# First expert stage: a quarter of the tokens by gathered expert rows, the rest dense with a token-stationary second product

## The chip, the cores and the metric

The kernel runs on one core of a Trainium2 chip. The metric is the device time of one execution in microseconds, as a median of runs; one execution was also recorded by the hardware profiler. PE is the tensor engine, DVE is VectorE, ACT is ScalarE, POOL is GpSimd, SP is SyncE, whose queue issues most transfers.

## The reference

Two blocks are computed in a row. The first has two layers over 256 context tokens and 256 latent tokens of width 1024; the second has four layers over 16 + 256 tokens and is not touched. Each layer of the first block ends with a product-key expert network (PEER). For a token h it picks 16 experts in each of 8 heads, 128 rows out of 16384, with softmax gates, and adds up their contributions:

```python
qr = (h @ wq).reshape(b, t, 8, 2, 128)
scores = einsum('bthpd,hpkd->bthpk', qr, subkeys)
s1, i1 = top_k(scores[..., 0, :], 16); s2, i2 = top_k(scores[..., 1, :], 16)
top, pos = top_k(s1[..., :, None] + s2[..., None, :], 16)   # over the 256 sums
eidx = take(i1 * 128 + i2, pos); gate = softmax(top)
act = gelu(einsum('ted,td->te', u[eidx], h))
y = einsum('te,ted->td', gate * act, v[eidx])
```

u and v have 16384 rows of 1024 numbers each. The first layer does this for 512 tokens, the second for 256.

## The kernel before

Activations lie transposed: features on the 128 partitions, tokens along the row, as eight chunks of 128 features. Products are exact to float32: each weight tile `[128, 1024]` is loaded (`wraw`), split into a high part (`whi`, ACT, L202) and a remainder (`wlo`, DVE, L269), the tokens are split likewise into `xh` and `xl`, and three matmuls (high by high, high by low, low by high) are added up in PSUM.

The expert network of a layer is the function `peer`. It is dense: all 16384 experts are computed for all tokens, as 128 groups j of 128 experts, and a gate of zero stands for an expert that was not chosen. It has two parts.

*Routing* (`route`) makes queries and scores on PE, picks the 16 largest on DVE (`choose`), normalises the gates (`gates`), and spreads them over all experts (`spread`): for each token two one-hot matrices are built on DVE (`oa`, `ob`) and multiplied on PE, with the gate in three bf16 parts in the first layer and in one float32 part in the second; the result goes to an array `G` in DRAM. The generator yields the assumed PE and DVE time of each step, and `peer` fills in whole groups of the first product (`u_act`) wherever DVE is assumed to be ahead. These early groups go to an array `U` in DRAM (108 of 128 in the first layer, 124 in the second).

*The dense stage* walks over pairs of groups. `u_phase` fetches gates (`gt`) and stored products (`ad`), or computes a late group itself, applies GELU and gate, and splits the result (`wt`). `v_phase` loads two tiles of v, splits them into `vh` and `vl`, and multiplies with v as the stationary operand and 512 tokens moving: 8 output chunks x 2 groups x 3 parts. In the first layer four output chunks stay in PSUM (the tag `SM`) for the whole stage and four are made in the rotating banks (`MM`) and added to an accumulator in SBUF by DVE (L948). `u_phase` of a pair comes ahead of `v_phase` of the pair before. One row of 1024 modulation weights rides along per pair (`extra`, the function `mods`, DVE at L396) until they are done. A tile scheduler sets the order on each engine; each engine takes its queue in order.

Of the kernel before, what the change touches and what calls it, by code (L numbers as in the profile page):

```python
# [10 lines left out]
F32 = mybir.dt.float32  # L11
# [51 lines left out]
class Big:  # L63
    """chunks x [128, n] in 8 KB pieces."""
# [14 lines left out]
class Kern:  # L79
    def __init__(self, tc, st, A):  # L80
# [7 lines left out]
        self.gdram = [self.dr.tile([P, n // GT, P, GT], F32, name=f"g{n}") for n in (512, 256)]  # L88
        self.udram = [self.dr.tile([P, P, n], F32, name=f"u{n}") for n in (512, 256)]
# [11 lines left out]
    # ---------------------------------------------------------------- constants  # L101
    def consts(self):
# [39 lines left out]
        # -1e30 where column > row; where row > column; off the causal part of the 16-blocks  # L142
# [22 lines left out]
        # hsel[p, h]: 1 at p = h, 32 + h, 64 + h, 96 + h  # L165
# [6 lines left out]
        # hsel16[p, h]: 1 at p = h of every 16  # L172
# [6 lines left out]
        # csel[:, 15 - r:31 - r]: ones in column r of 16  # L179
# [28 lines left out]
    def sigmoid(self, out, z):  # L208
        """1 / (1 + exp(-z))"""
# [52 lines left out]
    def load_w(self, src):  # L262
        """A weight tile [128, n <= 1024] as an exact sum of two float32r parts."""
# [12 lines left out]
    def linear(self, wap, kc, xh, xl, cols, mts, consume, order=None, after=None):  # L276
        """out^T[m-tile] = W[:, m-tile]^T @ x for x^T = xh + xl, [128, kc, tokens]."""
# [15 lines left out]
    def rsq(self, src, n, tag="t", v=None, out=None, eps=None):  # L293
        """(src / n + eps) ** -0.5; v: a tile to reuse; eps: by token"""
# [13 lines left out]
    def root(self, v, l, r):  # L308
        """v ** -0.5 in r; l: to work in"""
# [19 lines left out]
    def norm(self, x, cols, parts, xh, xl, off=0, sums=None):  # L329
        """parts: (a, b, gain [128, 8], shift [128, 8] or None) over column ranges of x."""  # L330
# [16 lines left out]
    # ---------------------------------------------------------------- block 1  # L347
# [10 lines left out]
    def mods(self, l, groups, wt="wmod", jt="j"):  # L358
        """groups: (stream, modulation index) pairs: self.mod[l, s, i] -> [128, 8] columns, tile by tile."""
# [48 lines left out]
    def lower(self):  # L408
        """lower bounds of layer 1: (p0 + p1) - p0 of the softmax over the layers."""
# [16 lines left out]
    def forget(self, l, d, h, ps, b, key):  # L426
        """forget gate of direction d, head h: decay sums b within 128-blocks and the key."""
# [3 lines left out]
        # without a lower bound the floor of the gate is a bound on z  # L431
# [17 lines left out]
    def transposed(self, src, out, blks=None, tag="SM"):  # L449
        """out[t, blk, 128] <- src [128, N] transposed by token blocks."""  # L450
# [14 lines left out]
    def att_levels(self, d, q, k, b, nb, att, levels, tag="SM"):  # L465
        """att[i][s, (h, t)] off the diagonal for direction d, level by level; q, k, b: [128, H, n] in nb blocks."""
# [35 lines left out]
    def state_step(self, d, k, b, blk, vn, S, Snew):  # L502
        """Snew = exp(b_last) S + (k exp(b_last - b))^T v over one block."""
# [1389 lines left out]
```

## Time and profile before

| | |
|---|---|
| median of 3 runs | 4804.88 us (4804.5 to 4808.62) |
| profiled execution: span | 4797.2 us |
| the median above that span | 7.7 us |
| PE busy | 4635.6 us, 97% |
| DVE busy | 3518.2 us, 73% |
| ACT busy | 2207.3 us, 46% |
| POOL busy | 1.0 us |
| moved by DMA | 797.59 MB, mean 166 GB/s |

By stage: the first layer's routing lies from about 340 to 1185 us of the span, its dense stage to 2036, the second layer's mixer to 2260, its routing to 2745, its dense stage to 3135, and the second block after that. Matmuls overlap: the duration of one is longer than its slot in a stream of them, so a slot is read from the starts of a series. Busy time in a stretch is counted once where instructions overlap.

### The profile page before, as it was taken

The numbers are of one execution on the slowest core, as the hardware profiler recorded it, in microseconds if no ns is written. First come the engines' busy times: TensorE is split into PE (matmuls) and PEld (weight loads), VectorE is DVE, ScalarE is ACT, GpSimd is POOL, SyncE is SP. The second block draws the span as 40 slices with busy tenths as digits, with TensorE's granted clock in tenths as the row PEclk, the third lists the DMA queues.
The fourth block names the chain that finished last, engine by engine and source line by source line (L and its number), as shares of the span: only waits on it lengthen the run. The fifth ranks groups of instructions, "written<-read, shape, count | busy, mean of one in ns | idle before, by whom it ended". The sixth has DMA issues, their size and how long they took to land.

```text
span 4797.2 us, 78132 instructions
## 1 busy us (share of the span) xinstructions
PE 4635.6 (97%) x30559; PEld 4149.6 (87%) x30559; DVE 3518.2 (73%) x6655; ACT 2207.3 (46%) x3847; POOL 1.0 (0%) x8
## 2 busy tenths in 40 slices
PE   7999899999999999999999999999999999999999
PEld 5887788888777778878999999978998998899799
DVE  9977998898887775487966866677557567566765
ACT  4443233334333332365445555577445454445853
POOL 0000000000000000000000000000000000000000
PEclk9999999999999999999999999999999998999999
DMA  5423345456867764224577788733553553055255
GB/s 191 131 69 99 102 173 179 167 181 234 263 222 229 228 204 133 80 74 132 182 224 233 265 294 275 239 95 102 173 157 99 174 160 106 15 173 167 89 167 172
DMA packets 317218, 797.59 MB, mean 166 GB/s; under 512 B 26272, under 2 KB 142368, under 8 KB 306608
## 3 DMA queue, kind: packets, MB, share of 16 engines
q1 hardware_dynamic: 316848, 792.60, 50.9%
q8 instruction: 239, 3.92, 0.3%
q14 instruction: 131, 1.07, 0.1%
HBM read 696.28 MB, written 95.94 MB: 165 GB/s over the span
## 4 chain that ended last, share of the span: by engine, by line
PE 77%; DVE 11%; DMA 6%; issue 3%; ACT 3%; SPq 0%; DVEq 0%; ACTq 0%
PE MM L287 32%; PE MM L868 21%; PE SM L942 10%; DMA wraw<-wmodT 4%; PE SM L830 3%; PE MM L942 2%; DVE vl L274 2%; PE A L490 2%; DVE wlo L269 1%; DMA ad<-u 1%; PE PO L1233 1%; DVE b L948 1%; DVE wt L274 1%; DVE j L396 1%; ACT whi L202 1%
## 5 line engine op out<-in xcount | busy, mean ns | idle before, releaser
L202 ACT ACTIVATE whi<-wraw 128x1024 fp32r<-128x1024 f32 (+2 forms) x796 | 831.5, 1046 | 1315.3 <-PE MM L868 650.1
L269 DVE TENSOR_TENSOR wlo<-wraw,whi 128x1024 fp32r<-128x1024 f32 (+2 forms) x796 | 956.0, 1202 | 311.0 <-ACT whi L202 223.2
L868 PE MATMUL MM<-b,whi 128*128 128x512 f32 (+1 forms) x4096 | 1015.9, 339 | 3.6 <-ACT whi L202 3.6
L287 PE MATMUL MM<-xhl,whi 128*128 128x272 f32 (+1 forms) x4736 | 936.4, 294 | 3.2 <-ACT xhl L202 1.6
L287 PE MATMUL MM<-b,whi 128*128 128x272 f32 (+2 forms) x3712 | 851.6, 323 | 50.4 <-ACT b L202 45.3
L287 PEld LDWEIGHTS MM<-xhl,whi 128*128 128x128 f32 x4736 | 752.8, 190 | 24.3 <-issue 10.5
L868 PEld LDWEIGHTS MM<-b,whi 128*128 128x128 f32 x4096 | 700.5, 190 | 81.7 <-ACT whi L202 5.4
L287 PEld LDWEIGHTS MM<-b,whi 128*128 128x128 f32 x3712 | 621.7, 192 | 105.5 <-ACT b L202 51.7
L868 PE MATMUL MM<-b,wlo 128*128 128x512 f32 (+1 forms) x2048 | 693.3, 339 | 13.9 <-DVE wlo L269 13.8
L287 PE MATMUL MM<-xhl,wlo 128*128 128x272 f32 (+1 forms) x2368 | 690.4, 292 | 2.1 <-DVE wlo L269 2.0
L942 PE MATMUL SM<-wt,vh 128*128 128x256 f32 (+1 forms) x3072 | 689.1, 320 | 2.1 <-ACT wt L202 2.1
L287 PE MATMUL MM<-b,wlo 128*128 128x272 f32 (+2 forms) x1856 | 596.8, 322 | 7.9 <-DVE wlo L269 7.5
L942 PEld LDWEIGHTS SM<-wt,vh 128*128 128x128 f32 x3072 | 515.3, 192 | 43.4 <-ACT wt L202 2.3
L942 PE MATMUL SM<-wt,vl 128*128 128x256 f32 (+1 forms) x1536 | 490.8, 320 | 0.0
L287 PEld LDWEIGHTS MM<-xhl,wlo 128*128 128x128 f32 x2368 | 450.0, 190 | 9.8 <-issue 4.7
L202 ACT ACTIVATE vh<-wraw 128x1024 fp32r<-128x1024 f32 x256 | 266.6, 1050 | 403.6 <-PE MM L942 260.3
L868 PEld LDWEIGHTS MM<-b,wlo 128*128 128x128 f32 x2048 | 388.9, 190 | 59.3 <-DVE wlo L269 17.5
L274 DVE TENSOR_TENSOR vl<-wraw,vh 128x1024 fp32r<-128x1024 f32 x256 | 310.3, 1220 | 124.7 <-ACT vh L202 124.6
L287 PEld LDWEIGHTS MM<-b,wlo 128*128 128x128 f32 x1856 | 355.4, 192 | 33.2 <-DVE wlo L269 12.3
L942 PE MATMUL MM<-wt,vh 128*128 128x512 f32 x1024 | 319.0, 393 | 26.5 <-DVE b L948 26.3
L942 PEld LDWEIGHTS SM<-wt,vl 128*128 128x128 f32 x1536 | 294.6, 192 | 20.7
L824 DVE SCALAR_TENSOR_TENSOR ob<-iotab,b,gp 128x384 bf16<-128x384 bf16 x512 | 282.2, 610 | 19.9 <-PE SM L830 19.9
(470 smaller groups left out, 5407.1 us busy)
## 6 DMA issues: line engine op xcount, KB each, us to landing
wraw<-uT SPq DMA_DIRECT2D x256, 512.0 KB, 3.6
wraw<-v SPq DMA_DIRECT2D x256, 512.0 KB, 4.6
wraw<-w_gate_up SPq DMA_DIRECT2D x176, 512.0 KB, 3.5
g<-b SPq DMA_DIRECT2D x48, 1024.0 KB, 6.0
wraw<-w_in SPq DMA_DIRECT2D x64, 512.0 KB, 3.5
gt<-g SPq DMA_DIRECT2D x32, 1024.0 KB, 7.3
wraw<-fox_w_in SPq DMA_DIRECT2D x64, 512.0 KB, 3.5
wraw<-w_down SPq DMA_DIRECT2D x64, 512.0 KB, 3.5
```

Source lines behind the costliest of these rows:

```text
L202: r = nc.scalar.activation(out, in_, func, **kw)
L269: nc.vector.tensor_sub(lo[:, :n], raw[:, :n], hi[:, :n].bitcast(F32))
L274: self.nc.vector.tensor_sub(lo, src, hi.bitcast(F32))
L287: nc.tensor.matmul(ps, w_, x_[k, slice(a, b)], start=(i == 0 and q == 0), stop=(i == kc - 1 and q == 2))
L396: q = nc.vector.scalar_tensor_tensor(j, w, 1.0, self.cond[:, s, :], op0=OP.mult, op1=OP.mult, accum_out=self.mod[l, s, i][:, k:k + 1])
L490: nc.tensor.matmul(p[:w, h * w:(h + 1) * w], xx, xx, start=True, stop=True)
L824: nc.vector.scalar_tensor_tensor(b_, iota[:, None, :].to_broadcast([P, parts, P]), i2T[:, t_], gp[:, :, t_].to_broadcast([P, parts, P]), o ...
L830: nc.tensor.matmul(pg[:, i * P:(i + 1) * P], a[:, i], b_[:, q], start=(q == 0), stop=(q == parts - 1))
L868: nc.tensor.matmul(ps, w_[:, k * P:(k + 1) * P], x_[k, slice(0, N)], start=(k == 0 and q == 0), stop=(k == KD - 1 and q == 2))
L942: nc.tensor.matmul(ps, w_[:, jj, c * P:(c + 1) * P], x_[:, jj], start=first, stop=end, skip_group_check=not own and N < 512)
L948: nc.vector.tensor_add(accs[c - 4, slice(0, N)], accs[c - 4, slice(0, N)], ps)
L1233: nc.tensor.matmul(po[rows, a:b], vn[:c1 - c0, ci * P + 64 * e:ci * P + 64 * e + 64], pT[:c1 - c0, ci * P:ci * P + w], start=(ci == 0), st ...
```

## The change

In the first layer 128 of the 512 tokens (the first 128 context tokens) leave the dense path (`FETCHED = (1, 0)`). For them `gates` computes the expert number i1 x 128 + i2 and keeps it with the gate (`fetch`); no one-hot matrices are made. In the dense stage `tokens_first` turns these tokens so that a token lies on a partition (`H`), and `fetched` goes over the 128 chosen experts of each token: POOL gathers for the 128 partitions the rows of u and v (one array `uv0` with both side by side, 8 KB a row) into one of five tiles `uv`; DVE forms the dot product of u and H with an accumulator (L874); ACT applies GELU and the gate; DVE adds the weighted v row to `o` (L867). Two such experts go with each pair of groups.

The other 384 tokens stay dense. `spread` uses the float32 one-hot form in both layers. In both layers the second product is turned: the tokens (`wt`) are stationary, 128 at a time, and 512 columns of v move; all of the output stays in PSUM for the whole stage (six banks in the first layer, four in the second), the accumulator in SBUF goes, and at the end the result is copied out, transposed on PE and added to x (`add`). v is read from the new array, where the rows of neighbouring partitions are 1 MiB apart instead of 512 KiB. `MM` has two banks instead of three, `wt` two buffers instead of three in the first layer's dense stage, and v's split shares the buffers `whi` and `wlo`, now three each. Comments were taken out, which moves line numbers. Code for a second layer with one dense tile (`whole`) isn't reached with these settings.

```diff
+FETCHED = (1, 0)
-WORKP = dict(nbig=2048, bufs=4, ga=3, w=(5, 2, 2), mm=3, sm=5)
-ROUTE = dict(bufs=8, t=4, gp=1, r=16, alt=2, oa=4, ob=12)
-DENSE = dict(bufs=1, gt=2, ad=2, vh=2, vl=2, wt=3)
+WORKP = dict(nbig=2048, bufs=4, ga=3, w=(5, 3, 3), mm=2, sm=6, sp=4)
+ROUTE = dict(bufs=7, t=4, r=16, alt=2, oa=4, ob=8)
+DENSE = dict(bufs=1, gt=2, ad=2, wt=2, o=2)
+OWN = dict(uv=5, H=1, ir=1)
...
+                if t < nf:
+                    fetch(t, *sels[t], g)
...
-                            nc.vector.scalar_tensor_tensor(
-                                b_, iota[:, None, :].to_broadcast([P, parts, P]), i2T[:, t_],
-                                gp[:, :, t_].to_broadcast([P, parts, P]), op0=OP.is_equal, op1=OP.mult)
...
+                        nc.vector.tensor_scalar(b_, self.iotaf, i2T[:, t_], gT[:, t_], op0=OP.is_equal, op1=OP.mult)
+                        nc.tensor.matmul(pg[:, i * P:(i + 1) * P], a[:, i], b_, start=True, stop=True)
...
+    def fetched(self, l, H, ids, g, acc):
...
+        def out(b):
+            for j in range(b, b + B):
+                v = uv.pop(j)[:, D:]
...
+                    nc.vector.scalar_tensor_tensor(acc, v, w[:, j:j + 1], acc, op0=OP.mult, op1=OP.add)
+                yield
+        for b in range(0, P, B):
+            for j in range(b, b + B):
+                z = uv[j] = self.t(2 * D, tag="uv")
+                nc.gpsimd.indirect_dma_start(z, None, self.A[f"uv{l}"],
+                                             bass.IndirectOffsetOnAxis(ap=ids[:, j:j + 1], axis=0))
+                nc.vector.scalar_tensor_tensor(self.t(D, BF, tag="ga"), z[:, :D], 1.0, H, op0=OP.mult, op1=OP.mult,
+                                               accum_out=act[:, j:j + 1])
...
+            self.actv(act[:, bs], act[:, bs], AF.Gelu)
...
+                self.actv(w[:, j:j + 1], act[:, j:j + 1], AF.Copy, scale=g[:, j:j + 1])
+            if b:
+                yield from out(b - B)
+        yield from out(P - B)
...
-        res = [self.ps() for _ in range(4)]
-        accs = self.big(4, 512) if N == 512 else None
+        res = [[self.ps() for _ in range(2)] for _ in range(nd)]
...
-                nc.sync.dma_start(raw, A["v"][l, :, j0 + jj, :])
-                self.split(raw, vh[:, jj], vl[:, jj])
...
+                nc.sync.dma_start(raw, A[f"uv{l}"].rearrange("(p j) d -> p j d", j=P)[:, j, D:])
...
+                for q, ws, v in ((0, (wh, wl), vh), (1, (wh,), vl)):
+                    for c in range(nd):
+                        for h in range(2):
+                            for i, w_ in enumerate(ws):
+                                nc.tensor.matmul(res[c][h], w_[:, jj, c * P:(c + 1) * P], v[:, h * 512:(h + 1) * 512],
+                                                 start=(j == 0 and q == 0 and i == 0), stop=(j == P - 1 and q == 1))
...
+                for _ in range(J):
+                    next(steps, None)
```

DVE in the first layer's dense stage, in the middle of the early pairs. Before, one pair: products with the gates (`ad`), remainders of v (`vl`) and of the weights (`wt`), the modulation work (`ga`, `mod`), and the additions to the accumulator in SBUF (`b`).

```order
L274 TENSOR_TENSOR vl<-wraw,vh 128x1024
L274 TENSOR_TENSOR wt<-ad,wt 128x1024
L274 TENSOR_TENSOR vl<-wraw,vh 128x1024
L396 SCALAR_TENSOR_TENSOR ga,mod_12740<-wraw,cond 128x1024
L396 SCALAR_TENSOR_TENSOR ga,mod_12741<-wraw,cond 128x1024
L948 TENSOR_TENSOR b_11290<-b_11290,MM 128x512
L918 TENSOR_TENSOR ad<-ad,gt 128x512 x2
L948 TENSOR_TENSOR b_11290<-b_11290,MM 128x512 x2
```

And now, one pair; the remainder of v has the name `wlo`, the dot product reads `uv` and `H`, the sum goes to `o`.

```order
L976 TENSOR_TENSOR ad<-ad,gt 128x384 x2
L279 TENSOR_TENSOR wlo<-wraw,whi 128x1024
L279 TENSOR_TENSOR wt<-ad,wt 128x768
L279 TENSOR_TENSOR wlo<-wraw,whi 128x1024
L401 SCALAR_TENSOR_TENSOR ga,mod_9515<-wraw,cond 128x1024
L401 SCALAR_TENSOR_TENSOR ga,mod_9516<-wraw,cond 128x1024
L874 SCALAR_TENSOR_TENSOR ga,sp<-uv,H 128x1024
L867 SCALAR_TENSOR_TENSOR o<-uv,sp,o 128x1024
L874 SCALAR_TENSOR_TENSOR ga,sp<-uv,H 128x1024
L867 SCALAR_TENSOR_TENSOR o<-uv,sp,o 128x1024
```

The additions out of PSUM are gone, and four instructions of 1024 columns, two of which read a gathered tile, stand ahead of the next pair's remainders.

PE in the same place. Before, part of one pair: each pair of high-part matmuls is followed by one of the remainder, per output chunk; chunks in `MM` are those that DVE adds up.

```order
L942 MATMUL SM<-wt,vh 128x512 x2
L942 MATMUL SM<-wt,vl 128x512
L942 MATMUL SM<-wt,vh 128x512 x2
L942 MATMUL SM<-wt,vl 128x512
L942 MATMUL MM<-wt,vh 128x512 x2
L942 MATMUL MM<-wt,vl 128x512
```

Now one pair of groups, and the first group of the next.

```order
L997 MATMUL SM<-whi,wt 128x512 x12
L997 MATMUL SM<-wlo,wt 128x512 x6
L997 MATMUL SM<-whi,wt 128x512 x12
L997 MATMUL SM<-wlo,wt 128x512 x6
L997 MATMUL SM<-whi,wt 128x512 x12
L997 MATMUL SM<-wlo,wt 128x512 x6
```

A group has 18 matmuls of 512 columns where it had 24, and its remainder is needed only after the twelfth.

POOL, whose queue held four index patterns at the start of the program and nothing later, now has all gathers in one row.

```order
L138 IOTA t 128x128
L872 DMA uv<-uv,sp 128x2048 x128
```

## Rows read from the trace of the kernel before

**Rows 1.** The page: the span, and part 1, busy us (share) and instructions.

```profile
span 4797.2 us, 78132 instructions
PE 4635.6 (97%) x30559; PEld 4149.6 (87%) x30559; DVE 3518.2 (73%) x6655; ACT 2207.3 (46%) x3847; POOL 1.0 (0%) x8
```

**Rows 2.** Busy time by stretch: length, PE, PEld, DVE, ACT, POOL, clock, DMA, GB/s.

```profile
340.00:1185.00 845.00, 826.41 (x4787) 679.10 (x4786) 733.23 (x1677) 294.86 (x568) 0.00 (x0) 0.99 0.46 159
1185.00:2036.00 851.00, 824.52 (x3581) 674.79 (x3580) 589.73 (x794) 279.53 (x304) 0.00 (x0) 0.99 0.61 197
...
2745.00:3135.00 390.00, 385.94 (x3197) 385.13 (x3196) 247.53 (x354) 210.70 (x286) 0.00 (x0) 1.00 0.81 265
```

**Rows 3.** Groups of DVE instructions, 1185 to 2036 us: busy, mean ns, idle before.

```profile
L948 DVE TENSOR_TENSOR b<-b,MM 128x512 f32<-128x512 f32 x252 | 168.0, 682 | 91.7 <-PE MM L942 91.4
...
L396 DVE SCALAR_TENSOR_TENSOR ga<-wraw,cond 128x1024 bf16<-128x1024 f32 x80 | 96.9, 1221 | 71.1 <-DMA wraw<-wmodT 69.8 <-DMA u<-ga 1.3
```

**Rows 4.** PE in order of time, second product of the first layer.

```profile
1504.05 0.62 PE L942 MATMUL SM<-wt,vh 128*128 128x512 f32 x2
...
1509.49 0.62 PE L942 MATMUL MM<-wt,vh 128*128 128x512 f32 x2
```

**Rows 5.** Busy time by stretch, second layer's dense stage (columns of rows 2).

```profile
2900.00:3000.00 100.00, 100.00 (x836) 100.00 (x835) 62.88 (x87) 54.03 (x70) 0.00 (x0) 1.00 0.84 274
```

**Rows 6.** DVE in order of time, first layer's dense stage.

```profile
1206.10 1.22 DVE L274 TENSOR_TENSOR wt<-ad,wt 128x1024 fp32r<-128x1024 f32 x1
1207.23 1.21 DVE L396 SCALAR_TENSOR_TENSOR ga<-wraw,cond 128x1024 bf16<-128x1024 f32 x1
1208.38 0.08 DVE L396 DVE_READ_ACCUMULATOR ga<-wraw,cond 128x1 f32 x1
```

**Rows 7.** DVE in order of time, first layer, gates being spread.

```profile
805.64 0.69 DVE L818 TENSOR_TENSOR oa<-iotab,b 128x512 bf16<-128x512 bf16 x1
806.25 2.21 DVE L824 SCALAR_TENSOR_TENSOR ob<-iotab,b,gp 128x384 bf16<-128x384 bf16 x4
808.36 0.69 DVE L818 TENSOR_TENSOR oa<-iotab,b 128x512 bf16<-128x512 bf16 x1
```

**Rows 8.** PE in order of time, first layer, gates being spread.

```profile
802.00 1.51 PE L830 MATMUL SM<-ob,oa 128*128 128x128 bf16 x24
803.33 0.70 PE L868 MATMUL MM<-b,whi 128*128 128x512 f32 x2
```

**Rows 9.** PE in order of time, second layer, gates being spread (two passes each).

```profile
2605.24 2.84 PE L830 MATMUL SM<-ob,oa 128*128 128x128 f32 x24
2607.83 0.48 PE L868 MATMUL MM<-b,whi 128*128 128x256 f32 x2
```

**Rows 10.** DVE in order of time, second layer, gates being spread.

```profile
2602.03 0.68 DVE L818 TENSOR_TENSOR oa<-iotaf,b 128x512 f32<-128x512 f32 x1
2602.64 1.11 DVE L828 TENSOR_SCALAR ob<-iotaf,b 128x128 f32<-128x128 f32 x4
2603.66 1.21 DVE L269 TENSOR_TENSOR wlo<-wraw,whi 128x1024 fp32r<-128x1024 f32 x1
```

**Rows 11.** Busy time by stretch: the program's start, the dense stage's start.

```profile
10.00:20.00 10.00, 4.83 (x22) 4.77 (x23) 7.00 (x52) 1.75 (x6) 0.00 (x0) 1.00 1.02 411
1200.00:1230.00 30.00, 30.00 (x135) 24.82 (x134) 29.95 (x44) 12.91 (x13) 0.00 (x0) 1.00 1.02 344
```

**Rows 12.** A gap of PE in order of time, and the stretch after it.

```profile
1289.15 0.73 PE L942 MATMUL MM<-wt,vh 128*128 128x512 f32 x2 [2.37 <-DVE b L948]
1290.00:1300.00 10.00, 10.00 (x39) 8.06 (x38) 8.56 (x12) 2.96 (x3) 0.00 (x0) 0.83 0.86 272
```

**Rows 13.** Transfers issued 1900 to 2030 us: count, size, median us to landing.

```profile
wraw<-v SPq DMA_DIRECT2D x9, 512.0 KB, 3.6
wraw<-uT SPq DMA_DIRECT2D x6, 512.0 KB, 3.6
```

**Rows 14.** Transfers of the whole program (columns of rows 13).

```profile
b<-wmodT SPq DMA_DIRECT2D x8, 1024.0 KB, 18.2
```

More of the change, by code (lines that the diff above doesn't have):

```diff
@@ L790, in gates @@
         def gates(t):
-            ts = slice(t * P, (t + 1) * P)
             with self.tc.high_priority():
@@ L846, in route, with tokens_first @@
                 yield from gates(t)
-            yield from spread(t)
+            if t >= nf:
+                yield from spread(t)
+    def tokens_first(self, xh, xl, t):
+        nc = self.nc
+        H, one = self.t(D, tag="H"), self.t(P, F32R, tag="ir")
+        nc.vector.tensor_copy(one, self.ident)
+        ts = slice(t * P, (t + 1) * P)
+        for h in range(2):
+            ps = self.ps("MM")
+            for k in range(4):
+                o = ps[:, k * P:(k + 1) * P]
+                nc.tensor.matmul(o, xh[4 * h + k, ts], one, start=True, stop=False)
+                nc.tensor.matmul(o, xl[4 * h + k, ts], one, start=False, stop=True)
+            self.actv(H[:, h * 512:(h + 1) * 512], ps, AF.Copy)
+        return H
+    def fetched(self, l, H, ids, g, acc):
+        nc = self.nc
+        act, w = self.t(P, tag="sp"), self.t(P, tag="sp")
+        uv, B = {}, 1
+        def out(b):
+            for j in range(b, b + B):
+                v = uv.pop(j)[:, D:]
+                if j == 0:
+                    nc.vector.tensor_scalar(acc, v, w[:, 0:1], None, op0=OP.mult)
+                else:
+                    nc.vector.scalar_tensor_tensor(acc, v, w[:, j:j + 1], acc, op0=OP.mult, op1=OP.add)
[7 more added lines that the diff above has]
+                                               accum_out=act[:, j:j + 1])
+            bs = slice(b, b + B)
+            self.actv(act[:, bs], act[:, bs], AF.Gelu)
+            for j in range(b, b + B):
+                self.actv(w[:, j:j + 1], act[:, j:j + 1], AF.Copy, scale=g[:, j:j + 1])
+            if b:
+                yield from out(b - B)
+        yield from out(P - B)
     def peer(self, l, extra=()):
@@ L860, in peer @@
         self.norm(x, cs, parts + [(T, 512, M(0, 4), M(0, 3))], xh, xl, off=cs[0])
-        G, U = self.gdram[l], self.udram[l]
+        whole = ND == P
+        if whole:
+            xw = self.t(KD * P, tag="xw").rearrange("p (k n) -> p k n", k=KD)
+            nc.vector.tensor_add(xw, xh.all3(KD)[:, :, dc].bitcast(F32), xl.all3(KD)[:, :, dc].bitcast(F32))
         def u_act(j, func):
-            hi, lo = self.load_w(A["uT"][l, j])
-            ps = self.ps("MM")[:, :N]
-            for k in range(KD):
+            ps = self.ps("MM")[:, :ND]
+            if whole:
+                raw = self.w.tile([P, 1024], F32, name="wraw", bufs=self.wb[0])
+                nc.sync.dma_start(raw, A["uT"][l, j])
+                for k in range(KD):
+                    nc.tensor.matmul(ps, raw[:, k * P:(k + 1) * P], xw[:, k], start=k == 0, stop=k == KD - 1)
+            else:
+                hi, lo = self.load_w(A["uT"][l, j])
+            for k in range(0 if whole else KD):
                 for q, (w_, x_) in enumerate(((hi, xh), (hi, xl), (lo, xh))):
-                    nc.tensor.matmul(ps, w_[:, k * P:(k + 1) * P], x_[k, slice(0, N)],
+                    nc.tensor.matmul(ps, w_[:, k * P:(k + 1) * P], x_[k, dc],
                                      start=(k == 0 and q == 0), stop=(k == KD - 1 and q == 2))
-            a = self.t(tag="ga")[:, :N]
+            a = self.t(tag="ga")[:, :ND]
             self.actv(a, ps, func)
@@ L1802, in layout @@
         DEPTH, P, P, D)
-    a["v"] = I["peer_v"].reshape(DEPTH, P, P, D)
+    for l in range(DEPTH):
+        a[f"uv{l}"] = np.concatenate([I["peer_u"][l], I["peer_v"][l]], axis=1)
     vec = []
@@ L1861, in program @@
                 with ExitStack() as s2:
-                    K.work(s2, **WORKP)
+                    K.work(s2, **{**WORKP, **(WHOLE if l and FETCHED[l] else {})})
                     K.peer(l, () if l else chain(K.mods(0, [(1, 5), (0, 5)], "wraw", "ga"), K.mods(
```

138 lines of the change are left out of this document (67 added, 71 removed).

## The prediction

> **What bounds the kernel now.** I read the page's busy times first: the tensor engine (PE) is busy 4635.6 of 4797.2 us [rows 1], so time leaves the kernel only where PE work leaves, or where something else takes its place as the bound. Then the busy times by stage [rows 2]. First-layer routing with its early experts (340 to 1185 us) has PE busy 826 of 845 us and VectorE (DVE) 733; the first dense stage (1185 to 2036) PE 825 of 851, DVE 590, the DMA engines 0.61 busy; the second layer's dense stage (2745 to 3135) PE 386 of 390. All three are PE-bound, so each is costed as a sum over PE work and then tested for what is late next. In the first dense stage something already sits close behind: one DVE group waited 69.8 us for modulation rows from memory [rows 3].
>
> **Prices.** A 512-column matmul takes a slot of 0.2267 us: 24 of them between 1504.05 and 1509.49 [rows 4]. At 256 columns it is 100 us / 836 = 0.1196 us [rows 5]. The trace has no 384 columns; I interpolate, 0.1732 us (bounds: 0.17 if the slot is pure proportion, 0.2267 if nothing is saved). DVE slots, start to start: 1024 columns of two float32 sources 1.13 us, with an accumulator 1.15 us [rows 6], 512 columns 0.61 us [rows 7]; by straight line 768 columns 0.87, 384 columns 0.48 us.
>
> **Routing, first layer.** Early experts fall from 108 to 80, as the order of the loads to and from the scratch array shows: before 108 x 24 x 0.2267 = 588 us of PE, after 80 x 24 x 0.1732 = 333 us. The spreading matmuls change form: 24 bf16 ones (8 tokens) took 802.00 to 803.33, 0.166 us a token [rows 8]; 24 float32 passes (12 tokens) 2605.24 to 2607.83, 0.216 us a token [rows 9]. 512 x 0.166 = 85 against 384 x 0.216 = 83 us: nothing. So PE loses 255 us here, 826 to 571. Is DVE then the bound? Spreading four tokens took 2.72 us (805.64 to 808.36 [rows 7]) and will take 1.63 us (2602.03 to 2603.66 [rows 10]): 128 x 2.72 - 96 x 1.63 = 192 us less; 28 weight remainders less, 32 us. DVE goes from 733 to about 509, 0.89 of PE as before, so the old idle of 19 us should stay. The third PSUM buffer of the products is gone too; I price that at nothing, since a result has a whole expert, 4.2 us, to be copied out. **Routing: -255 us**, to 590.
>
> **Dense stage, first layer.** The loop goes over 64 pairs of experts; 40 now find their first product in memory, 24 don't. PE per pair: 36 slots of 512 columns, 8.16 us, instead of 48, 10.88; a late pair adds 48 x 0.1732 = 8.31, so 16.47. DVE per early pair: two remainders of v 2.26, remainder of the weights 0.87, two gate products 0.96, and new: two dots 2.30 and two sums into the output 2.26: 8.65 us. The modulation work that rides along (80 products [rows 3]: 24 weight rows for two streams, then 32 for one) adds 2.30 us in the first 24 pairs and 1.15 in the next 32. So 10.95 and 9.80 us in early pairs, above PE's 8.16, and 11.0 to 12.2 in late ones, below PE's 16.47. (The removed PSUM additions, 252 x 0.682 us [rows 3], pay for half of the new DVE work.)
>
> Transfers per early pair, in millions of bytes: v 1.05, two gathers 2.10, gates and stored products 0.79, modulation 0.52: 4.46. The engines moved 344 GB/s while full with this stage's mix, which has 512-byte pieces, and 411 GB/s at the start of the program with long rows only [rows 11]. That is 12.95 or 10.84 us a pair: as much as DVE or more. A late pair moves 5.11, 14.9 us at the lower rate: hidden under PE. Gathers bring 8 KB rows, but the small pieces stay, and the dots stand in DVE's in-order queue: a late gather holds up the remainders of v and the modulation products behind it, and PE behind those. So nearer the slow end: 12.4 us. **40 x 12.4 = 496 us.** Late pairs at PE's 16.47, with the 3% of stalls that PE has in this stage today: 24 x 17.0 = 408. The ends (the token rows of H, two experts left over, the result's transposes) have no row; they lie between nothing and 64 small DVE slots of 0.48 us, 31 us, and I take the middle, 15 us. **919 against 851: +68 us.**
>
> PE will idle some 4 us in each early pair, and that costs clock: after a gap of 2.37 us the granted clock was 0.83 over ten us [rows 12], full speed with about 3.4 us at the lower of its two levels, 1.7 us of work lost. One or two such gaps bring PE to 9.9 or 11.6 us a pair, still under 12.4: covered, but without slack.
>
> **Second layer.** Its second product turns token-stationary too: 24 x 0.1196 = 2.87 us an expert becomes 12 x 0.2267 = 2.72, -19 us over 128; the ends cost some 7. **-12 us.**
>
> **Sum.** 4797.2 - 255 + 68 - 12 = 4598 us of span. The median of the runs is 7.7 us above the span; on that scale **4606 us**.
>
> **Two rules weighed.** Loads of v now step through memory at 1 MiB from partition to partition, before at 512 KiB. Rows: in a quiet stretch v and uT, whose rows lie end to end, both land in 3.6 us [rows 13], so 512 KiB costs nothing here. The Trainium skill (DMA: Bandwidth & Descriptors, Latency and other measured facts) gives 207 GB/s for row pitches of 512 KiB and 164 for 2 MiB; the trace does not agree at 512 KiB. By an estimate between the two, 185 GB/s, a v load would take 2.8 us and the sum would be about 4880 us. The other is in the skill's page SBUF — State Buffer (Who interferes with whom): a DVE instruction with two SBUF inputs and a GpSimd instruction that reads SBUF shut each other out. No row of before has a gather; if each of the 80 early ones costs DVE one more slot, 1.15 us, that is 92 us, 4698, inside rival two.
>
> **Rivals.**
> *One, the transfers hide.* At 411 GB/s DVE alone sets the early pairs: 24 x 10.95 + 16 x 9.80 = 420, late 395, ends 15: dense 830. 4797.2 - 255 - 21 - 19 = 4502, **about 4510**. For it: long rows. Against: today's stage already waits on memory at 0.61 busy.
> *Two, waits add instead of overlapping.* Low rate plus the two dots that can't begin before their rows: 12.95 + 2.30 = 15.3 us, 40 x 15.3 + 24 x 17.5 + 15 = 1047, +196, no gain in layer two: **about 4745**. For it: one in-order queue per engine, five row buffers, two of them in use.
> *Three, slower.* The wider pitch makes every v load hold the transfer engines longer by x us. 80 loads in early pairs pay at once; 48 in late pairs have about 1 us each to spare, the 128 of layer two 0.31 (0.84 busy of 2.87 us against 2.72). 256x - 88 us passes the 199 gained at x = 1.1: v at 2.5 us a load, where today's rates make it 1.3 to 1.5. At x = 1.4 it is **4876**. Rows 13 speak against it.
> *Four, slower gathers.* At three in flight, one landing every 8.6 us would make the dense stage 1100 us and undo everything; that needs 26 us from issue to landing. The worst 1 MB loads today land in 18.2 us, behind a queue of many [rows 14].
>
> **How the numbers follow.** Forecast 0.52, rival one 0.17, two 0.16 (partial mixes with three included), three 0.07, four 0.05, no visible change 0.03. The forecast's own range, from 11.4 to 13.6 us an early pair and 384 columns at 0.170 to 0.185 us, is 4555 to 4690. For 8 in 10 it reaches to rival one's 4510 and past rival two's 4745: **4510 to 4760**. 0.2%, some 10 us, is what a measurement of this kernel can tell from no change. Faster 0.84, same 0.04, slower 0.12.
>
> **What the changed profile would show.** Routing about 590 us long with PE still at 0.97. Dense about 920: its first 40 pairs near 12.4 us with PE two thirds busy, DVE over 0.85, transfers near full, PE waiting for v's remainders; its last 24 near 17 with PE full. Second-layer dense 12 to 19 us shorter. I am wrong if the early pairs stand far from 12.4 us, if v lands later than uT in quiet stretches, if POOL's gathers issue late, or if DVE slots beside a gather grow beyond 1.15 us.

## The result and the profile after

The changed kernel took 4655.15 us, the median of 4 runs (4650.69 to 4658.39), beside 4805.09 us for the kernel before on the same chip: a ratio of 0.9686, interval 0.9672 to 0.9699. That lies inside the range, 49 us above the predicted time. The profiled execution's span went from 4797.2 us [rows 1] to this (the page):

```profile
span 4655.8 us, 72086 instructions
PE 4348.6 (93%) x27548; PEld 3924.8 (84%) x27548; DVE 3428.6 (74%) x6645; ACT 2215.4 (48%) x4048; POOL 176.6 (4%) x136
```

PE lost 287 us of work, but the span only 141: 146 us came back as PE waiting, 4 points of its share. Where, the busy times by stretch tell (columns of rows 2): first-layer routing, the whole first dense stage, its early pairs, its late pairs, the second layer's dense stage.

```profile
340.00:955.00 615.00, 579.68 (x3354) 541.12 (x3353) 504.86 (x1476) 234.18 (x446) 7.14 (x5) 0.98 0.50 167
955.00:1868.00 913.00, 793.70 (x3531) 672.00 (x3530) 729.49 (x979) 353.39 (x626) 168.43 (x123) 0.93 0.87 319
960.00:1400.00 440.00, 337.07 (x1272) 264.16 (x1270) 374.14 (x508) 156.64 (x281) 94.72 (x70) 0.87 0.96 354
1500.00:1760.00 260.00, 260.00 (x1325) 237.72 (x1324) 197.17 (x253) 108.89 (x189) 40.56 (x32) 1.00 0.86 313
2595.00:2990.00 395.00, 364.42 (x1588) 287.38 (x1587) 227.50 (x318) 191.22 (x261) 0.00 (x0) 1.00 0.76 242
```

A pair of groups is early when its first product lies in memory already (40 of the 64 pairs), and late when the stage makes it itself (24). Set against [rows 2]: routing went from a PE at 0.98 to 0.94, the late pairs are PE alone, the early pairs leave PE idle for 103 of 440 us beside transfer engines at 0.96 busy, and the second layer, 386 of 390 before, now has 364 of 395. The stages' lengths come from the first and last starts of PE's matmuls by line: the second product (line 997) in each layer, and the first product (929) where the late pairs begin.

```profile
L997 PE MATMUL SM<-whi,wt x1536: 387/389/792, 959.6 to 1854.7; 128*128 128x512 f32 x192
L997 PE MATMUL SM<-wlo,wt x768: 387/389/797, 962.4 to 1856.1; 128*128 128x512 f32 x192
...
L997 PE MATMUL SM<-whi,wt x1024: 387/389/754, 2579.5 to 2985.1; 128*128 128x512 f32 x171
L997 PE MATMUL SM<-wlo,wt x512: 388/389/629, 2583.0 to 2986.1; 128*128 128x512 f32 x171
...
L929 PE MATMUL MM<-b,whi x484: 333/334/443, 1434.6 to 1699.9; 128*128 128x384 f32 x162
```

The first layer's second products run from 959.6 to 1856.1, 896.5 us; 1380 of its 2304 matmuls, 38.33 pairs of 36, lie before 1434.6, so an early pair takes 475.0 / 38.33 = 12.39 us. The second layer's run 406.6 us, before 381.8 (2749.7 to 3131.5). Taken from each stage's first matmul to the next stage's:

| stretch | predicted | before to after, us | measured |
|---|---|---|---|
| up to the first early product | 0 | 385.8 to 388.4 | +2.6 |
| routing, first layer | -255 | 804.0 to 571.2 | -232.8 |
| dense stage, first layer | +68 | 843.8 to 904.6 | +60.8 |
| mixer between | 0 | 227.9 to 231.6 | +3.7 |
| second layer, routing and dense | -12 | | -4.5 + 24.8 = +20.3 |
| rest of the program | 0 | | +4.1 |
| sum (rounded) | -199 | 4797.2 to 4655.8 | -141.4 |

One term has the wrong sign: the second layer's. Part of an early pair shows how the waits are built (order of time, all engines; a bracket is the idle time before, and what ended it):

```profile
1105.64 0.33 SPq L990 DMA_DIRECT2D wraw<-uv  x1
...
1107.87 1.22 DVE L874 SCALAR_TENSOR_TENSOR ga<-uv,H 128x1024 bf16<-128x1024 f32 x1
...
1111.24 1.06 ACT L207 ACTIVATE whi<-wraw 128x1024 fp32r<-128x1024 f32 x1 [6.30 <-DMA wraw<-uv]
1112.20 0.94 ACT L207 ACTIVATE sp<-sp 128x1 f32<-128x1 f32 x4
1112.75 1.28 DVE L867 SCALAR_TENSOR_TENSOR o<-uv,sp,o 128x1024 f32<-128x1024 f32 x1 [3.65 <-ACT sp L207]
1113.95 1.02 DVE L976 TENSOR_TENSOR ad<-ad,gt 128x384 f32<-128x384 f32 x2
...
1114.89 1.22 DVE L279 TENSOR_TENSOR wlo<-wraw,whi 128x1024 fp32r<-128x1024 f32 x1
...
1116.16 2.93 PE L997 MATMUL SM<-wlo,wt 128*128 128x512 f32 x6 [6.77 <-DVE wlo L279]
```

ScalarE waits 6.30 us for v. Behind that split, in its in-order queue, stand the small Gelus of the fetched tokens (sp), so VectorE's sum waits 3.65 us although its rows have landed (the dot before it read them); v's remainder (wlo) comes behind the sum, and PE has by then waited 6.77 us. Between 960 and 1430 such waits add up to (us in total, times, longest):

```profile
ACT whi L207 <- DMA wraw<-uv: 148.3, 39, 6.3
PE SM L997 <- DVE wlo L279: 108.7, 33, 7.4
DVE o L867 <- ACT sp L207: 29.8, 12, 3.8
```

In the second layer there are no gathers, and still v lands late (transfers of 2595 to 2975: count, size, median us to landing):

```profile
wraw<-uv SPq DMA_DIRECT2D x118, 512.0 KB, 7.5
ad<-u SPq DMA_DIRECT2D x28, 512.0 KB, 7.2
gt<-g SPq DMA_DIRECT2D x28, 512.0 KB, 6.5
```

Before, in that stage (2750 to 3120), stored products took 6.0 us, gates 5.2, and v:

```profile
wraw<-v SPq DMA_DIRECT2D x124, 512.0 KB, 4.9
```

The waits of the changed kernel in the same stretch (columns as above):

```profile
ACT ad L207 <- DMA ad<-u: 174.6, 28, 8.4
DVE ad L976 <- ACT ad L207: 136.8, 28, 6.9
...
PE SM L997 <- ACT whi L207: 21.2, 21, 2.4
```

Before (2750 to 3133), ScalarE waited little for stored products, and PE not at all for the split of v:

```profile
ACT ad L202 <- DMA ad<-u: 20.7, 20, 2.0
```

Two theories. **A**: the rows of v, now 1 MiB apart, land late. **B**: the edit also took the split activations (wt) from three buffers to two, so stored products are freed, and loaded, late. (The section on the change names this for the first layer only; the setting holds in both.) For the early pairs: is it the transfers, VectorE, or the order in which the queues wait?

### The profile page after: what moved, and what is told of

Its sections match the earlier page's. It is cut to its first block, busy times and chain, and to the rows that moved or that the text cites. A ratio compares the mean times of both kernels' runs of the same rounds, so it can differ in the third digit from the quotient of the medians.

```text
span 4655.8 us, 72086 instructions
## 1 busy us (share of the span) xinstructions
PE 4348.6 (93%) x27548; PEld 3924.8 (84%) x27548; DVE 3428.6 (74%) x6645; ACT 2215.4 (48%) x4048; POOL 176.6 (4%) x136
## 4 chain that ended last, share of the span: by engine, by line
PE 53%; DMA 11%; DVE 8%; ACT 6%; issue 2%; SPq 0%; ACTq 0%; DVEq 0%
PE MM L292 27%; PE MM L929 11%; PE SM L997 6%; DMA wraw<-uv 5%; DMA ad<-u 5%; ACT whi L207 3%; DVE wlo L279 1%; PE PO L1296 1%; DVE wlo L274 1%; PE SM L821 1%; PE A L495 1%; DVE wt L279 1%; ACT wt L207 1%; DVE o L867 1%; PE A L1799 0%
## 5 line engine op out<-in xcount | busy, mean ns | idle before, releaser
L207 ACT ACTIVATE whi<-wraw 128x1024 fp32r<-128x1024 f32 (+1 forms) x1052 | 1098.3, 1048 | 1418.2 <-PE MM L292 508.1
L929 PE MATMUL MM<-b,whi 128*128 128x384 f32 (+1 forms) x4096 | 902.9, 311 | 7.8 <-ACT ga L207 5.9
L292 PEld LDWEIGHTS MM<-xhl,whi 128*128 128x128 f32 x4736 | 755.0, 191 | 24.8 <-issue 10.3
L997 PE MATMUL SM<-whi,wt 128*128 128x512 f32 x2560 | 658.1, 403 | 38.5 <-ACT whi L207 25.5
L929 PE MATMUL MM<-b,wlo 128*128 128x384 f32 (+1 forms) x2048 | 636.8, 311 | 16.1 <-DVE wlo L274 16.0
L997 PEld LDWEIGHTS SM<-whi,wt 128*128 128x128 f32 x2560 | 496.4, 196 | 164.6 <-ACT whi L207 35.9
L997 PE MATMUL SM<-wlo,wt 128*128 128x512 f32 x1280 | 361.7, 416 | 110.8 <-DVE wlo L279 110.5
L292 PEld LDWEIGHTS MM<-xhl,wlo 128*128 128x128 f32 x2368 | 451.7, 191 | 12.4 <-DVE wlo L274 6.5
L997 PEld LDWEIGHTS SM<-wlo,wt 128*128 128x128 f32 x1280 | 251.9, 200 | 179.2 <-DVE wlo L279 126.8
L279 DVE TENSOR_TENSOR wlo<-wraw,whi 128x1024 fp32r<-128x1024 f32 x256 | 310.4, 1222 | 104.6 <-ACT whi L207 94.9
L872 POOL DMA_INDIRECT uv<-uv,sp x128 | 175.6, 1372 | 1632.0 <-DVE ob L820 892.8
L867 DVE SCALAR_TENSOR_TENSOR o<-uv,sp,o 128x1024 f32<-128x1024 f32 x127 | 162.9, 1282 | 30.4 <-ACT sp L207 30.4
```

Source lines behind the costliest of these rows:

```text
L207: r = nc.scalar.activation(out, in_, func, **kw)
L279: self.nc.vector.tensor_sub(lo, src, hi.bitcast(F32))
L292: nc.tensor.matmul(ps, w_, x_[k, slice(a, b)], start=(i == 0 and q == 0), stop=(i == kc - 1 and q == 2))
L867: nc.vector.scalar_tensor_tensor(acc, v, w[:, j:j + 1], acc, op0=OP.mult, op1=OP.add)
L872: nc.gpsimd.indirect_dma_start(z, None, self.A[f"uv{l}"], bass.IndirectOffsetOnAxis(ap=ids[:, j:j + 1], axis=0))
L929: nc.tensor.matmul(ps, w_[:, k * P:(k + 1) * P], x_[k, dc], start=(k == 0 and q == 0), stop=(k == KD - 1 and q == 2))
```

## The experiments

Totals are medians of 4 runs; the kernel before took 4799.95 to 4806.65 us beside them, so totals a few us apart are no difference. "Early pair" and the two stages are read from the starts of matmuls, as above. Kernels 3 and 4 leave work out. The expectations for 1, 3 and 4 give the changed kernel's early pair as 12.7 us and its first dense stage as 904.6, which runs to the mixer's first matmul; those for 5 to 9 give the early pair as 12.2. By the count above it is 12.39, and the table's stage ends with the last second product, 896.5.

| kernel | total | ratio to before (interval) | early pair | first dense | second dense |
|---|---|---|---|---|---|
| changed | 4655.15 | 0.9686 (0.9672 to 0.9699) | 12.39 | 896.5 | 406.6 |
| 1 v's own array | 4627.62 | 0.9640 (0.9624 to 0.9656) | 12.20 | 888.0 | 387.4 |
| 2 wt x3, layer two | 4641.53 | 0.9665 (0.9649 to 0.9681) | 12.44 | 896.4 | 400.3 |
| 3 no gathers | 4578.19 | 0.9538 (0.9522 to 0.9554) | 10.72 | 822.9 | 404.1 |
| 4 no sums | 4606.15 | 0.9601 (0.9585 to 0.9617) | 11.34 | 847.1 | 404.5 |
| 5 = 1 + 2 | 4628.12 | 0.9631 (0.9614 to 0.9647) | 12.18 | 886.5 | 388.8 |
| 6 = 5, pace 1 and 4 | 4595.05 | 0.9563 (0.9547 to 0.9579) | 9.53 | 857.0 | 386.4 |
| 7 = 5, pace 1.5 and 3 | 4612.88 | 0.9600 (0.9584 to 0.9616) | 10.91 | 872.6 | 386.6 |
| 8 60 ahead | 4635.06 | 0.9641 (0.9625 to 0.9657) | 12.47 | 939.0 | 404.7 |
| 9 = 1, pace 1 and 3, 60 ahead | 4590.24 | 0.9553 (0.9535 to 0.9571) | 9.59 | 915.8 | 388.3 |
| 10 v end to end | 4620.44 | 0.9619 (0.9599 to 0.9640) | 12.23 | 887.1 | 381.1 |
| 11 = 10, pace 1 and 4, ad and gt x3 | 4592.77 | 0.9552 (0.9536 to 0.9567) | 9.55 | 857.8 | 380.5 |
| 12 = 10, pace 1 and 4, loads ahead | 4595.05 | 0.9567 (0.9550 to 0.9584) | 9.69 | 860.3 | 383.9 |

**1. v from its own array**

```diff
-nc.sync.dma_start(raw, A[f"uv{l}"].rearrange("(p j) d -> p j d", j=P)[:, j, D:])
+nc.sync.dma_start(raw, A["v"][l, :, j])
...
+a["v"] = I["peer_v"].reshape(DEPTH, P, P, D)
```

> The changed kernel with v read from its own array, rows 512 KiB apart as before the change, instead of from the halves of the joined array, rows 1 MiB apart; the gathers still read the joined array. Theory A (the 1 MiB pitch is why v now lands in 6.7 to 7.4 us and why the second layer's dense stage takes 406.6 us where it took 381.8): v lands in about 5 us in the second layer, its dense stage goes back by 10 to 25 us, the early pairs of the first layer go from 12.7 to about 12 us, total about 4615 to 4640 us. Theory B (the later landing is a queue behind loads that are issued in bursts, because one buffer of w fewer frees the tiles late): v's landing stays within 0.5 us of the changed kernel's and the total within 5 us of 4655.

The second layer's stage lost 19.2 us, the first's 8.5, and v lands sooner in the second (2585 to 2945):

```profile
wraw<-v SPq DMA_DIRECT2D x117, 512.0 KB, 6.2
gt<-g SPq DMA_DIRECT2D x28, 512.0 KB, 5.4
ad<-u SPq DMA_DIRECT2D x27, 512.0 KB, 6.5
```

A holds for 19 of the 25 us; the landing went to 6.2, not to the 5 expected, nor back to the 4.9 that v took at the same distance before, and the other loads of the stage, whose own addresses did not change, land about a microsecond sooner too. Early pairs gain just 0.19 us. The array's place in memory changes together with the distance; that it is the distance rests on kernel 10, which goes on in the same direction.

**2. Three buffers of wt in the second layer**

```diff
-self.part(dense, **DENSE, **(OWN if nf else {}))
+self.part(dense, **{**DENSE, "wt": 2 if nf else 3}, **(OWN if nf else {}))
```

> The changed kernel with three buffers of the split gated activations (wt) in the second layer's dense stage, as before the change, instead of two; the first layer is not touched. Theory B (the second layer lost its 25 us because a tile of the stored products is freed only when the split into a wt buffer can run, so its successor is loaded late): the second layer's dense stage goes from 406.6 to 382 to 392 us, total 4630 to 4642. Theory A (pitch of v): within 4 us of 4655.

Its stage lost 6.3 us, between the two forecasts (the kernels with rows 1 MiB apart that leave this layer alone, changed, 3, 4 and 8, lie 404.1 to 406.6). The rest of the total's difference lies outside it and has no cause here.

**3. No gathers**

```diff
-v = uv.pop(j)[:, D:]
+v = uv[j % 5][:, D:]
...
-z = uv[j] = self.t(2 * D, tag="uv")
-nc.gpsimd.indirect_dma_start(z, None, self.A[f"uv{l}"],
...
+if j < 5:
+    uv[j] = self.t(2 * D, tag="uv")
+    nc.gpsimd.indirect_dma_start(uv[j], None, self.A[f"uv{l}"],
...
+z = uv[j % 5]
```

> Leaves out 123 of the 128 gathers: five tiles of expert rows are fetched once and every dot and every sum reads one of these, so VectorE, ScalarE and TensorE do the same work on the wrong rows. If transfers set the early pairs of the first layer's dense stage (DMA busy 0.92 to 1.02 there, 1 MiB of 4 to 4.5 MiB per pair is gathered, twice that per two pairs), the early pairs go from 12.7 to about 10 to 11 us (PE busy 8.2, VectorE about 10.8 per pair) and the stage from 904.6 to about 835 to 860 us; if VectorE or the order on the engines sets them, the stage stays within 10 us of 904.6. The second layer is not touched: within 3 us.

10.72 us a pair, as the first forecast had it, and 74 us off the stage, slightly more than it had. In the early pairs (960 to 1400) it is VectorE that is full, 429 of 440 us, the transfers at 0.68:

```profile
960.00:1400.00 440.00, 372.31 (x1525) 296.14 (x1524) 429.24 (x579) 185.82 (x329) 0.00 (x0) 0.95 0.68 220
```

**4. No sums**

```diff
-else:
-    nc.vector.scalar_tensor_tensor(acc, v, w[:, j:j + 1], acc, op0=OP.mult, op1=OP.add)
```

> Leaves out 127 of the 128 weighted sums on VectorE (line 867); gathers, dots, Gelus and weights are kept, so the transfers are the same and VectorE does 2 x 1.28 us less for each pair. If VectorE sets the early pairs, they go from 12.7 to about 10.5 us and the stage from 904.6 to about 810 to 840 us; if transfers do, early pairs stay within 0.4 us of 12.7 and the stage within 20 us of 904.6; the late pairs, where PE is busy all the time, gain nothing in either case. The second layer is not touched: within 3 us.

11.34 us a pair, between the two forecasts, and 49 us off the stage. The edit does more than take work from VectorE: its waits for the small Gelus go too, and a gathered tile is free as soon as its dot is done. Now the transfers are full and VectorE is not:

```profile
960.00:1400.00 440.00, 355.08 (x1396) 275.50 (x1395) 321.21 (x481) 169.50 (x313) 128.99 (x79) 0.93 1.02 392
```

So either alone would need some 10.7 us (VectorE) or 11.3 us (transfers) a pair; neither is full in the changed kernel (0.85 and 0.96), and what is above the larger of them, about 1 us a pair, is left to the queues that wait in order (argued; no run isolates it).

**5. Both repairs of the second layer** (the diffs of 1 and 2 together)

> Both repairs of the second layer at once: v from its own array at 512 KiB from row to row, and three buffers of the split activations in the second layer. Alone, the first took 19 us from that layer's dense stage and the second 6. If they are two causes of the same loss, the stage comes to 380 to 384 us, what it took before the change, and the total to 4615 to 4622 us; if the array alone is the cause and the third buffer only hid part of it, the stage stays at 385 to 388 us and the total at 4622 to 4630 us.

388.8 against 387.4 us: once v has its own array, the third buffer gains nothing, so it had only hidden part of the array's cost. Theory B falls; the 6 us that are still missing to the 381.8 of before are kernel 10's subject.

**6 and 7. The fetched tokens paced**

```diff
-for _ in range(J):
+for _ in range(1 if j0 < early else 4):
     next(steps, None)
```

> As the kernel with both repairs, and the 128 steps of fetched tokens, two a pair throughout in the changed kernel, are paced at one in each early pair and four in each late pair. Transfers per early pair fall from 4.46 to 3.41 million bytes, VectorE's work there by 2.5 us. If the early pairs are set by transfers and VectorE as they stand (12.2 us a pair now, 10.5 with the gathers' transfers left out, 11.3 with the sums left out), they go to 9.5 to 10.2 us, 80 to 100 us in all; the late pairs, 16.5 us of PE, then hold some 15.8 to 16.6 us of VectorE work and 7.2 million bytes, 18.8 us at 383 GB/s, and become transfer-bound at 19 to 20.5 us: 60 to 95 us back. Total 4600 to 4640 us, little or no gain. If the in-order waits on v set the early pairs and not the amount of work, early pairs stay above 11.5 us and the total rises above 4640 us.

In kernel 7 the early pairs take `1 + j0 // J % 2` steps, the late ones 3:

> As the kernel with both repairs, with one and two steps of fetched tokens in turn in the early pairs (1.5 a pair) and three in each late pair. Early pairs carry 3.94 million bytes and about 9.7 us of VectorE work, late pairs 6.16 million bytes, 16.1 us at 383 GB/s, beside 16.5 us of PE. If early pairs are set by the amount of transfers and VectorE's work: 11.0 to 11.4 us a pair, 30 to 45 us less, and late pairs stay within 0.5 us of 16.5: total 4580 to 4595 us. If in-order waits set them: total within 10 us of the kernel with both repairs.

Early pairs came out at 9.53 and 10.91 us, so it is mostly the amount of work that sets them. Kernel 6's total came out below its forecast, kernel 7's above. Late pairs went to 485.4 / 25 = 19.4 us with four steps, as expected, and 17.9 with three, where the forecast had them within 0.5 us of PE's 16.5: that was wrong. Between 1420 and 1720 PE waited 22.9 us there for the remainders of u that VectorE makes, with VectorE busy 243 of 300 us and the transfers at 0.89: neither was full. In kernel 6 transfers are at 0.94 or more all through the stage, early and late:

```profile
965.00:1330.00 365.00, 329.64 (x1378) 260.68 (x1377) 319.34 (x437) 153.01 (x231) 43.11 (x40) 0.98 0.98 358
1420.00:1720.00 300.00, 263.91 (x1241) 236.75 (x1239) 251.28 (x327) 112.63 (x238) 77.50 (x60) 0.94 0.94 351
```

**8. Fewer experts done ahead**

```diff
-HEAD = (10.0, 0.0)
+HEAD = (-30.0, 0.0)
```

> The changed kernel, with 60 experts' first products done ahead in routing instead of 80 (the start value of the balance of costs is -30 instead of 10). If routing is bound by PE, it loses 20 x 24 x 0.1733 = 83 us; VectorE, busy 505 of 615 us there, would leave at most some 60. In the dense stage ten pairs turn from early (12.2 us) to late (16.5 us): 43 us more. Total 4610 to 4650 us, a gain of 5 to 40 us, if early pairs are as bound by transfers as they look: then a product done ahead buys only 4.3 us of dense time a pair for 8.3 us of PE time in routing. If products done ahead were still worth their time, the total would rise above 4660 us.

Routing ended at 898.0 us of the span instead of 959.6, 61.6 sooner, and the dense stage grew by 42.5: a gain, as forecast. An expert done ahead costs more than it saves while early pairs are bound by something else than PE.

**9. Three edits together** (the diffs of 1 and 8, and 6's with three steps for four)

> Three edits that each gained alone, together: v from its own array, one step of fetched tokens in an early pair and three in a late one, and 60 experts done ahead in place of 80. If their gains are of separate stages, routing takes 512 us as with 60 ahead alone, and the dense stage about 30 x 9.6 + 34 x 17.9 + some 15 = 910 us (9.5 and 17.9 us a pair measured with one and with three steps); with the second layer at 387 us the total is 4570 to 4585 us. If the dense stage is by now set by its transfers as a whole (0.94 to 0.97 busy when paced at one and four), the 20 products moved into it bring 6.5 million bytes more, 18 us, and the stage stays nearer 880 us: 4545 to 4565 us. If gains overlap and 60 ahead no longer pays once early pairs are cheap, 4590 us or more.

Total as kernel 6, within what can be told, as the third forecast had it: once early pairs are down to 9.6 us, routing's 60 us come back in the dense stage (915.8 against 857.0). The gains of 8 and of the pacing do not add up.

**10. v end to end**

```diff
+nc.sync.dma_start(raw, A["v"][l, j])
+a["v"] = np.ascontiguousarray(I["peer_v"].reshape(DEPTH, P, P, D).transpose(0, 2, 1, 3))
```

> The changed kernel with v in an array of its own in which the 128 rows of one load lie end to end, 4 KB from partition to partition, where the changed kernel has 1 MiB and the kernel with v's own array 512 KiB (these landed in 7.2 to 7.5 us and 6.2 us in the second layer). If the distance between rows is what costs, and 512 KiB is not yet free under load, v lands in 4.8 to 5.5 us as uT does, the second layer's dense stage goes below 387 us, to 370 to 384, the early pairs of the first layer to 11.5 to 11.9 us, and the total to 4600 to 4618 us. If only the wider step costs, everything is as with v's own array: 387 us and 4622 to 4632 us.

The second layer's stage falls by another 6.3 us, to 381.1, as the first forecast had it; the first layer's stays, early pairs at 12.23 us included, which it had not. v lands in 5.9 us there, where 4.8 to 5.5 were expected:

```profile
wraw<-v SPq DMA_DIRECT2D x117, 512.0 KB, 5.9
```

The total is not told apart from kernel 1 by its interval, but the stage is: 386.4 to 388.8 us in the five kernels with v at 512 KiB (1, 5, 6, 7, 9), 380.5 to 383.9 in the three with its rows end to end (10, 11, 12). PE's waits left in that stage (2575 to 2950):

```profile
PE SM L997 <- DVE wt L279: 5.9, 15, 0.4
PE SM L997 <- ACT whi L207: 4.6, 7, 1.5
```

**11 and 12. What holds the last 10 us**

Both stand on 10 and 6's pacing. Kernel 11 gives the second layer three buffers each of stored products (ad) and gates (gt); kernel 12 has two, and issues both loads (`stored`) one step of four groups earlier instead. The first two lines are kernel 11's, the rest is kernel 12's:

```diff
-self.part(dense, **DENSE, **(OWN if nf else {}))
+self.part(dense, **{**DENSE, **({} if nf else {"ad": 3, "gt": 3})}, **(OWN if nf else {}))
...
+held.update(held.pop("next", None) or stored(j0))
+if j0 + 4 < P:
+    held["next"] = stored(j0 + 4)
```

> What gained so far, put together: v with its rows end to end, one step of fetched tokens in an early pair and four in a late one; and, in the second layer's dense stage only, three buffers each of stored products and of gates in place of two. With the rows of v end to end that stage still had 10.5 us of TensorE waiting (4.6 for the split of v on ScalarE, which stands behind Gelus that wait for stored products, 127 us of ScalarE's waits; 5.9 for the split of the activations). If the stored products are late because their buffer is freed late, a third one takes most of it: 370 to 375 us for the stage, against 381. If ScalarE's and VectorE's order holds it, 379 to 382. Total 4572 to 4588 us.

> As the kernel with v's rows end to end and the steps paced at one and four, two buffers each of stored products and gates; but both are loaded one group of four experts earlier in the program, before the v loads of the group in hand. If the Gelus on stored products wait because those loads stand late in the queue behind bursts of v loads (114 to 127 us of ScalarE's waits in the second layer's dense stage), these waits go below 40 us, TensorE's 10 to 15 us of waits there below 6, and the stage from 381 to 371 to 375 us. If not the place in the queue but the time in flight holds them, the stage stays at 379 to 382 us. In the first layer's dense stage transfers are full, so it should stay within 8 us of 857. Total 4575 to 4585 us by the first, 4588 to 4596 us by the second.

380.5 and 383.9 us: neither helped, and in kernel 12 ScalarE still waits 138.1 us for stored products. So it isn't the number of buffers and not the place in the program alone. Kernel 12's order of time shows a load issued only when VectorE has split products of the step in hand (2710.59, 0.69 us), and the next Gelu waiting for it:

```profile
2706.03 0.63 ACT L207 ACTIVATE ad<-ad 128x512 f32<-128x512 f32 x1 [6.35 <-DMA ad<-u]
...
2710.59 0.69 DVE L279 TENSOR_TENSOR wt<-ad,wt 128x512 fp32r<-128x512 f32 x1
...
2711.30 0.34 SPq L967 DMA_DIRECT2D ad<-u  x1
...
2716.88 1.15 ACT L207 ACTIVATE ad<-ad 128x512 f32<-128x512 f32 x2 [4.85 <-DMA ad<-u]
```

Two buffers with the earlier load may simply be too few, and both edits together weren't tried. Nor was a rival that the same stretch (2560 to 2915) names: the queue that issues the loads waits 192.9 us for VectorE's remainders of v, before it can issue v's next tiles, and the stored products stand in that queue too. This stays open.

## Why the prediction was right, and where it was wrong

The span came out 58 us above the forecast 4598: 22 us from routing, 32 from the second layer and 10 from stretches priced at nothing, less 7 from the first dense stage.

**Routing, -255 predicted, -232.8 measured.** The prices held: 384 columns take 0.173 us a slot, the value interpolated (the starts of each three are 0.52 us apart: 639.92, 640.44, 640.96), and spreading four tokens takes VectorE 1.63 us (699.59 to 701.22), the row used. PE's work fell by 247 us, 8 less than priced, for which no row gives a cause. The step that missed most is "the old idle of 19 us should stay": PE was idle 35 us of 615. Fifteen of these lie between 700 and 960 us, where VectorE begins full (columns of rows 2); before, PE was busy without a break from 570 to 1190. I had judged VectorE's share by its mean over the stage. Of PE's waits between 700 and 959 us, 9.2 us are for VectorE's work (the remainders of u and the one-hot `ob`), and another 4.9 for ScalarE. No run tests what a lighter VectorE would give back.

```profile
700.00:800.00 100.00, 96.54 (x624) 94.14 (x623) 99.99 (x251) 43.13 (x96) 0.00 (x0) 1.00 0.56 194
800.00:900.00 100.00, 96.04 (x668) 92.52 (x666) 88.02 (x247) 48.81 (x126) 0.00 (x0) 1.00 0.51 188
900.00:960.00 60.00, 52.34 (x318) 50.31 (x319) 38.97 (x89) 23.61 (x50) 7.14 (x5) 0.94 0.83 297
```

```profile
PE MM L929 <- DVE wlo L274: 6.1, 10, 1.2
PE SM L821 <- DVE ob L820: 3.1, 8, 0.5
```

**Dense, first layer, +68 predicted, +60.8 measured.** The bounds were right: transfers and VectorE near each other, PE idle a quarter of the early time. An early pair took 12.39 us for 12.4; a late one PE's own time: 84 matmuls a pair and 1325 in 260 us make 16.5, without the 3% of stalls that I added. These leave 13 us for the ends, priced at 15. Kernels 3 and 4 show a floor each, and that the rivals of pure hiding (10.5 us) and pure adding (15.3 us) are both wrong.

The reason given for "nearer the slow end" was wrong, though: a late gather was to hold up VectorE's queue. No dot waited for its rows (the 0.0 below; 1216 to 1230 ns for each of the 128). What came late was v: ScalarE waited 148.3 us for it, the small Gelus stood behind, and VectorE's sums and PE waited in turn. And 12.4 was a choice between 10.84 and 12.95, not a sum: the transfers alone took 11.34 in kernel 4, and some 1 us of waits came on top. That the choice met the measured value so closely is luck in part.

PE's gaps cost clock (0.87 over the early pairs). That the waits cover this, as the prediction said, is argued: in kernel 6, where PE runs at 0.98 there, most of the gain is in the waits (PE's for wlo went from 108.7 to 25.0 us). The other part of rival two, gathers that block VectorE, is not seen: the dot (1024 columns of two sources) takes 1222 ns on average in the changed kernel and 1216 in the kernel without gathers.

```profile
L874 DVE SCALAR_TENSOR_TENSOR ga<-uv,H 128x1024 bf16<-128x1024 f32 x71 | 86.7, 1222 | 0.0
```

```profile
L876 DVE SCALAR_TENSOR_TENSOR ga<-uv,H 128x1024 bf16<-128x1024 f32 x81 | 98.4, 1216 | 0.0
```

The Trainium skill (SBUF — State Buffer, Who interferes with whom) says that a VectorE instruction with two SBUF inputs, as the dot is, and a GpSimd instruction that reads SBUF shut each other out; no run here shows it beside these gathers.

**Second layer, -12 predicted, +20.3 measured.** This is the step that failed: it was a sum of PE work only, in the stage with the fullest transfers of [rows 2] (0.81 busy). The wider step of v was weighed, from [rows 13], in a quiet stretch, where 512 KiB cost nothing; nothing there tells of a stage with transfers at 0.8. The dense stage missed its term by 37 us. The wider distance makes 19.2 of them (406.6 to 387.4 with v at 512 KiB, as before the change); rows end to end, which the kernel before did not have either, take off 6.3 more (381.1). PE still waits 10.5 us there, and without these it would take 370.6, the 369.8 of the term. So the price of PE's work held; that PE would be fed without waits, as it was before at 512 KiB, did not, and why not is open beyond the distance. Routing's -4.5 in that layer was not foreseen and is not explained.

**Rival three** had the place half right and the price wrong. It wanted 1.1 us more engine time a load, in the early pairs and in the second layer; going back to 512 KiB gave the early pairs 0.19 us each, the second layer's stage 19 us. What is seen there is a load that lands 1.3 us later (7.5 against 6.2), while the engines move nearly as much when busy; the rows are the changed kernel's and kernel 1's:

```profile
2595.00:2975.00 380.00, 350.65 (x1521) 276.49 (x1521) 220.45 (x299) 182.73 (x242) 0.00 (x0) 1.00 0.78 250
2585.00:2945.00 360.00, 344.86 (x1521) 276.10 (x1520) 220.69 (x298) 183.02 (x241) 0.00 (x0) 1.00 0.77 261
```

By an estimate from them, 95 million bytes at 250 / 0.78 instead of 261 / 0.77 GB/s over 118 loads, a load holds the engines 0.1 to 0.2 us longer. It comes to 35 us in all with rows end to end (4655 to 4620), not 280. What delays the landing is not seen. The Trainium skill (DMA: Bandwidth & Descriptors, Latency and other measured facts) has large powers of two as slow row distances, for tiles with 16 KiB a row: 207 GB/s at 512 KiB and 164 at 2 MiB, where it calls 214 full. Under load the runs agree with its direction at 512 KiB, and at 1 MiB, for which the page has no figure. My estimate by its figures, 4880 us, was far off: it took 185 GB/s for the rate of a load. Had I taken the ratio of 185 to 214, the load's 1.4 us would have grown by 0.2, an estimate from the same figures, near what is worked out above.

## What to carry to other kernels

A change that gives one array a second reader by joining it to another changes the row distance for the first reader too: cost it in the stage with the fullest transfers, not in a quiet one. Work spread evenly over a loop whose iterations have different bounds is worth placing by what each has spare: one fetched step in an early pair and four in a late one, one line of code, took 30 us or so off (kernel 6 against 5). Work done ahead (products kept in memory) is worth its time only where the engine it relieves is the bound later (kernel 8).

The versions at 4590 to 4595 us (6, 9, 11 and 12) are faster than both kernels, at 0.955 to 0.957 of the kernel before, and can't be told from each other.

## What had not been expected of the hardware

Rows 1 MiB apart land later under load than rows 512 KiB apart (7.5 and 6.2 us; 19 us of a stage). Rows 512 KiB apart and rows end to end land alike in a quiet stretch (3.6 us [rows 13]), and nearly so under load (6.0 to 6.2 us in five kernels, 5.8 to 6.4 in three), and yet the stage takes 386.4 to 388.8 us with the one and 380.5 to 383.9 with the other. Transfers that share the time with such a load land later themselves: gates 6.5 us beside rows 1 MiB apart, 5.4 beside 512 KiB. A gather of 128 rows of 8 KB landed in 8.8 us (median, early pairs) with five tiles in use, and no dot waited for one.
